# A two-block transformer kernel on one core: the second block's tail as tasks, its first up products by token rows, and several orders rewritten

## The chip, the cores and the metric

The kernel runs on one core of a Trainium2 chip. The core has a matrix engine (TensorE, PE in the profile, with its weight loads as PEld), a vector engine (VectorE, DVE), a scalar engine (ScalarE, ACT), a general one (GpSimd, POOL), and SyncE (SP), which here issues the DMA transfers. Each engine works off its own queue in order, and waits where an operand is not there yet. The metric is the device time of one execution in microseconds (us); the kernel before has a median of 1060.82 us over three runs (1060.1 to 1063.39).

## The reference

One sequence of 256 tokens, 1024 wide, in f32, passes through two blocks. Each block is modulated by vectors that come from a conditioning vector `c`: six vectors of 1024 for each block.

```python
# first block (hybrid_layer)
mod = silu(c) @ ada_w + ada_b
sh1, sc1, gt1, sh2, sc2, gt2 = split(mod, 6)
h = rmsnorm(x, mix_pre_g) * (1 + sc1) + sh1
z, xbc, dt_raw, sc_b, sc_c, sc_h, gates = split(h @ w_in)
y_ssd = ssd_branch(z, xbc, dt_raw, ...) @ w_ssd_out      # chunked scan, chunks of 128 tokens
y_sc = (sc_b * causal_dwconv(sc_c * sc_h, sc_conv_w)) @ w_sc_out
x = x + gt1 * rmsnorm((g_ssd * y_ssd + g_sc * y_sc) @ w_o, mix_post_g)
h = rmsnorm(x, ffn_pre_g) * (1 + sc2) + sh2
u_gate, u_val = split(causal_dwconv(h @ w_up, ffn_conv_w, ffn_conv_b))
x = x + gt2 * rmsnorm((silu(u_gate) * u_val) @ w_down, ffn_post_g)
# second block, "the companion" (hybrid_layer_2)
shift_a, scale_a, gate_a, shift_f, scale_f, gate_f = split(silu(c_2) @ w_ada_2 + b_ada_2, 6)
h = rms_norm(x, attn_norm) * (1 + scale_a) + shift_a
o_a = nsa_mixer(...)       # 8 heads: compressed, selected and windowed keys
o_b = mla_mixer(...)       # 8 heads from low-rank q and kv
x = x + gate_a * ((g_a * o_a + g_b * o_b) @ w_o_2)
h = rms_norm(x, ffn_norm) * (1 + scale_f) + shift_f
val, gt = split(causal_conv3(h @ w_up_2) + b_conv)       # 2 x 2816 channels
x = x + gate_f * ((silu(gt) * val) @ w_down_2)
```

In the kernel the companion's vectors are called sha, sca, ga, shf, scf, gf, in this order.

## The kernel before, in words

**Weights.** All weights are f32 and pass once from DRAM, in halves of 128x1024 values (512 KB), into `raw` buffers (six of them) on SP's queue. ACT rounds each half to the matrix format (`hi`), DVE makes the rest (`lo` = `raw` minus `hi`); five pairs may be held at a time (`HALVES`). Activations exist as such pairs too (`h3h` and `h3l`, `h4h` and `h4l`, `osh` and `osl`, and so on). Each product is then three matrix products: hi by hi, lo by hi, hi by lo. Two forms occur: in the one the weights are stationary and all 256 tokens move, so the result has channels on the partitions; in the other a token tile of 128 is stationary and 512 weight columns move, so the result has tokens on the partitions.

**Order.** A planner in Python (`_Order`, from line 258) writes the program. Pieces of work are generators ("tasks") with a rank (`RANK`); `charge` adds an estimated duration to an engine's clock at each instruction, `pump` (line 323) emits the due task of lowest rank between products, and `force` (line 335) emits the earliest when the products wait. What comes out is a fixed order for each engine. The list `keys` (lines 736 to 769) sets the order of the weight chunks: `SSD_ORDER` for the scan, `ATT` for the attention, and `mix_in` (line 754) puts the chunks of a modulation vector between them, every so many chunks. All compute instructions go through line 408, so the profile shows them by tile names.

**Modulation vectors.** Most vectors need eight halves of their weight matrix, and `ada_mul` (line 966) takes each as one dot product on DVE (the instruction on `raw` and `crow`, shown as CUSTOM_DVE_ANT_0 in the profile and as ISA in the order). Those in `ON_PE`, gt2 and gf, are loaded separately: `adp_load` (line 994) puts eight halves into `big` buffers, `adp_add` (line 1006) sums part of them on DVE, seven of the eight for gf, and `adp_fill` (line 1023) ends the sum with f32 products on TensorE, which also spread it over all partitions.

**Tails.** Behind w_o, w_down and w_o_2 a "tail" scales the result by its gate, adds it to the residual `xr`, takes the norm, turns the tile to channels on partitions, applies scale and shift and makes the next `h` pair. `tail` (line 1495) emits it step by step from hand-written lists (`TAILS`): `mul` and `upd` on DVE, `sqx` on ACT, `nrm`, `diag` (a diagonal matrix `btok` of the norms), `turn` (f32 products of `xr` with `btok`, which scale and transpose in one), `evA` and `evV` (evictions with scale and shift on ACT or DVE), `hi`, `lo`. `out_proj` (line 677) runs the products ahead of it: the last two chunks are held, so that token tile 0 is ready ahead of tile 1.

**The end of the attention.** `mla_task` (line 2207) makes softmax rows `Sm` and `om`; sums go to `oA`, `os_task` (line 2414) splits them into `osh` and `osl`, the operand of w_o_2. Its first two chunks need only the first half of the heads, so their products lie between the last attention pieces. Then come the ga tail, up2 with 22 pairs of channel blocks (`ffn`, line 1671) and dn2.

Of the kernel before, what the change touches and what calls it, by code (L numbers as in the profile page):

```python
# [28 lines left out]
ON_PE = ("gt2", "gf")  # L29


def _plan():
# [70 lines left out]
    for i in range(22):  # L103
        plan.append((("up2", i), 2048, a_pair("w_up_2", 128 * i, 2816 + 128 * i)))
# [102 lines left out]
def _consts():  # L207
# [10 lines left out]
    for dim, s in ((128, ""), (64, "64")):  # L218
# [195 lines left out]
def _body(ctx: ExitStack, tc: tile.TileContext, wst, pf_d, rows_d, cst_d, xT_d, x_d, w2_d, out_d):  # L414
# [86 lines left out]
    st = {"dma": 0, "cast": 0, "half": 0, "ahead": 0}  # L501
# [23 lines left out]
    def cast_next():  # L525
# [30 lines left out]
    def caster():  # L556
        while st["cast"] < 2 * len(keys):
            yield lambda: st["ahead"] < limit[0] and st["cast"] in raws
# [118 lines left out]
    def out_proj(name, nch, x, ready, tail_of, done=lambda c: None):  # L677
# [12 lines left out]
        for c in range(nch - 2):  # L690
            ready(c, 0)
            ready(c, 1)

# [4 lines left out]
            done(c)  # L698
        held = []
        for c in (nch - 2, nch - 1):  # L700
# [3 lines left out]
        for t in range(2):  # L704
            for c in (nch - 2, nch - 1):
                ready(c, t)
            for j in range(2):
                for w, c, hf in held:
# [1771 lines left out]
```

## Time and profile before

| | |
|---|---|
| median of three runs | 1060.82 us (1060.1 to 1063.39) |
| the profiled execution, its own time | 1063.29 us |
| its span, first to last instruction | 1061.5 us |
| mean granted clock of TensorE | 0.988 |
| PE busy | 1027.2 us (97%) |
| PEld busy | 945.2 us (89%) |
| DVE busy | 847.2 us (80%) |
| ACT busy | 625.8 us (59%) |
| POOL busy | 37.1 us (3%) |
| DMA | 234.01 MB, mean 220 GB/s |

The profile is one execution. "Busy" counts the time in which an engine had an instruction in work. Matrix products overlap, so the price of one is read from start to start of a run of them, and not from its duration. The granted clock of a stretch is 1.00 at 2.4 GHz and 0.50 at 1.2 GHz. A row of the list of instructions may join several of one kind (x4), and "[2.79 <-ACT h4h L408]" says that the engine was idle for 2.79 us before it and that ACT's instruction on h4h ended the wait.

### The profile page before, as it was taken

How to read it: one execution, taken by the hardware profiler on the slowest of the kernel's cores; microseconds unless marked ns; L12 is line 12 of the kernel's file. 1: busy time of each engine (PE TensorE's matmuls, PEld its weight loads, DVE VectorE, ACT ScalarE, POOL GpSimd, SP SyncE). 2: the span in 40 equal slices, each digit the busy share in tenths (PEclk: the TensorE clock that was granted, in tenths of full speed). 3: DMA queues.
4: the chain of work that ended last, by engine and by line, in shares of the span. 5: the costliest groups of instructions: out<-in, count | busy, mean ns of one | idle time of the engine just before them, and what ended most of it. 6: DMA issues, size and time to landing. Idle time of an engine off the chain costs nothing.

```text
span 1061.5 us, 18723 instructions
## 1 busy us (share of the span) xinstructions
PE 1027.2 (97%) x7101; PEld 945.2 (89%) x7101; DVE 847.2 (80%) x1557; ACT 625.8 (59%) x1228; POOL 37.1 (3%) x59
## 2 busy tenths in 40 slices
PE   9899999999999999999998989998999789999998
PEld 8889999989999979999987779887998679999986
DVE  5888897978987867989886898997889677877843
ACT  4466577467754456656555467777764346666531
POOL 0000000000000000000000010221100000000000
PEclk8999999999999999999999999998999899999999
DMA  9955496657868947686785688853256716555551
GB/s 354 350 197 182 160 308 230 233 197 267 288 216 275 329 139 235 231 274 203 230 310 186 210 303 292 299 178 131 100 177 232 283 54 206 181 180 183 194 179 40
DMA packets 66186, 234.01 MB, mean 220 GB/s; under 512 B 7568, under 2 KB 8624, under 8 KB 65584
## 3 DMA queue, kind: packets, MB, share of 16 engines
q1 hardware_dynamic: 66096, 232.82, 64.1%
q8 instruction: 55, 0.90, 0.3%
q14 instruction: 35, 0.29, 0.1%
HBM read 230.67 MB, written 2.13 MB: 219 GB/s over the span
## 4 chain that ended last, share of the span: by engine, by line
PE 66%; DVE 6%; ACT 4%; issue 2%; DMA 1%; POOL 0%; SPq 0%; ACTq 0%; DVEq 0%; POOLq 0%
PE ps L408 66%; DVE lo L408 2%; DMA adp<-in_wst_dram 1%; ACT hi L408 1%; ACT S L408 1%; DVE raw L408 1%; DVE S L408 1%; ACT jk L408 0%; DVE jk L408 0%; DVE ropet L408 0%; ACT junk L408 0%; DVE qo L408 0%; DVE Sm L408 0%; POOL ssk L408 0%; DVE tmp L408 0%
## 5 line engine op out<-in xcount | busy, mean ns | idle before, releaser
L408 DVE TENSOR_TENSOR lo<-raw,hi 128x1024 fp32r<-128x1024 f32 (+3 forms) x326 | 387.4, 1195 | 153.0 <-ACT hi L408 150.5
L408 ACT CAST hi<-raw 128x1024 fp32r<-128x1024 f32 (+3 forms) x326 | 331.7, 1030 | 210.2 <-PE ps L408 153.9
L408 PE MATMUL ps<-hh,hi 128*128 128x256 f32 (+1 forms) x520 | 150.4, 291 | 3.1 <-ACT hh L408 3.1
L408 PE MATMUL ps<-hl,hi 128*128 128x256 f32 (+1 forms) x520 | 146.9, 284 | 0.7 <-DVE hl L408 0.2
L408 PE MATMUL ps<-hh,lo 128*128 128x256 f32 (+1 forms) x520 | 146.5, 283 | 0.1
L408 PEld LDWEIGHTS ps<-hh,hi 128*128 128x128 f32 (+1 forms) x520 | 98.6, 190 | 6.6 <-ACT hh L408 5.0
L408 PE MATMUL ps<-h4h,hi 128*128 128x256 f32 x352 | 99.8, 286 | 2.8 <-ACT h4h L408 2.8
L408 PEld LDWEIGHTS ps<-hl,hi 128*128 128x128 f32 (+1 forms) x520 | 98.7, 190 | 3.7 <-DVE hl L408 2.0
L408 PE MATMUL ps<-h4h,lo 128*128 128x256 f32 x352 | 99.6, 286 | 0.0
L408 PEld LDWEIGHTS ps<-hh,lo 128*128 128x128 f32 (+1 forms) x520 | 98.6, 190 | 0.4 <-DVE lo L408 0.3
L408 PE MATMUL ps<-h2h,hi 128*128 128x256 f32 x352 | 98.4, 283 | 0.0
L408 PE MATMUL ps<-h2h,lo 128*128 128x256 f32 x352 | 98.3, 283 | 0.0
L408 PE MATMUL ps<-h2l,hi 128*128 128x256 f32 x352 | 94.7, 283 | 0.0
L408 PE MATMUL ps<-h4l,hi 128*128 128x256 f32 x352 | 94.5, 283 | 0.0
L408 DVE CUSTOM_DVE_ANT_0 raw<-raw,crow 128x1024 f32<-128x1024 f32 x64 | 76.9, 1217 | 0.0
L408 DVE SCALAR_TENSOR_TENSOR fc<-ps,pf,fc 128x254 f32<-128x254 f32 (+1 forms) x176 | 72.3, 473 | 0.0
L408 PEld LDWEIGHTS ps<-h4h,hi 128*128 128x128 f32 x352 | 68.7, 195 | 3.0 <-ACT h4h L408 3.0
L408 PEld LDWEIGHTS ps<-h4h,lo 128*128 128x128 f32 x352 | 68.7, 195 | 0.0
L408 PEld LDWEIGHTS ps<-h2h,hi 128*128 128x128 f32 x352 | 67.6, 192 | 0.8 <-ACT h2h L408 0.8
L408 PEld LDWEIGHTS ps<-h2h,lo 128*128 128x128 f32 x352 | 67.6, 192 | 0.0
L408 PEld LDWEIGHTS ps<-h2l,hi 128*128 128x128 f32 x352 | 65.4, 192 | 0.0
L408 PEld LDWEIGHTS ps<-h4l,hi 128*128 128x128 f32 x352 | 65.4, 192 | 0.0
(393 smaller groups left out, 2330.8 us busy)
## 6 DMA issues: line engine op xcount, KB each, us to landing
raw<-in_wst_dram SPq DMA_DIRECT2D x364, 512.0 KB, 5.0
adp<-in_wst_dram SPq DMA_DIRECT2D x16, 512.0 KB, 7.3
ada0a<-in_wst_dram SPq DMA_DIRECT2D x8, 512.0 KB, 9.0
ada0b<-in_wst_dram SPq DMA_DIRECT2D x8, 512.0 KB, 9.1
E<-scr SPq DMA_DIRECT2D x4, 1024.0 KB, 8.8
raw<-in_wst_dram SPq DMA_DIRECT2D x8, 400.0 KB, 8.9
raw<-in_wst_dram SPq DMA_DIRECT2D x8, 384.0 KB, 8.8
brow<-in_rows_dram SPq DMA_DIRECT2D x4, 512.0 KB, 8.3
```

What stands on the lines that cost most here:

```text
L408: return f(*a, **k)
```

## The change

- gf is no longer in `ON_PE`. Its eight halves go through the weight stream as dot products on DVE, mixed into up2 from chunk 10, and eight small f32 products spread the result (`cst,mod_gf`). The separate loads, seven DVE steps and four wide f32 products of gf go.
- The ga tail is written as tasks (`tail_tasks`). ACT and DVE scale the rows by their norm into `tmp`, and eight plain transposes for each token tile (`cst,tmp`) take the place of the products with `btok`.
- w_o_2 holds all four chunks: token tile 0 runs over all of them, then tile 1. Halves beyond the five pairs go to `big` buffers (`whi`, `wlo`).
- The first four pairs of channel blocks of up2 come as two "windows" of token-row products (weights 512 wide, moving; new layout "up2b"): tile 0 for both windows, then tile 1. Four ACT copies (`ux`) and 16 transposes bring the result to channels on partitions; the rest is as before (`ffn2`).
- The order of the scan's chunks, of some attention chunks, the mixing of sc2, sha, sca, scf and shf, the ranks of many tasks, and a few steps in the lists of gt1 and gt2 are rewritten. shf moves from the attention's start into dn of the first block; scf's eight dot products come in a row.

```diff
-ON_PE = ("gt2", "gf")
+ON_PE = ("gt2",)
...
-    for i in range(22):
+    for p in range(2):
+        cols = np.concatenate([np.arange(256) + o + 256 * p for o in (0, 2816)])
+        for h in range(2):
+            plan.append((("up2b", p, h), 2048, b_list("w_up_2", 4 * h, 4, cols)))
+    for i in range(4, 22):
         plan.append((("up2", i), 2048, a_pair("w_up_2", 128 * i, 2816 + 128 * i)))
...
+SPARED = 3
+RANK_TAIL = (-1.5, -1.2)
...
+            inner = st["hl"] < HALVES
+            if inner:
+                h, l = hlp.tile([128, 1024], F32R, name="hi"), hlp.tile([128, 1024], F32R, name="lo")
+                st["hl"] += 1
+            else:
+                h, l = big("whi", F32R), big("wlo", F32R)
+                O.keep("big", 2)
+            home[i, hf] = inner
...
-    def out_proj(name, nch, x, ready, tail_of, done=lambda c: None):
+    def out_proj(name, nch, x, ready, tail_of, done=lambda c: None, hold=2, spared=None):
...
+        more[0] = spared
         held = []
-        for c in (nch - 2, nch - 1):
+        for c in range(nch - hold, nch):
             def mm(w, hf, c=c):
                 held.append((w, c, hf))
             step((name, c), mm, hold=True)
         for t in range(2):
+            for w, c, hf in held[:-4]:
+                if not hf:
+                    ready(c, t)
+                if not t:
+                    arrive(w, hf)
+                half(t, w, c, hf)
+                if t:
+                    drop(w.i, hf)
+                    if hf:
+                        done(c)
...
-    SSD_ORDER = [(x[:-1], int(x[-1])) for x in "z0 xs1 sc0 sc1 xs2 z1 sc2 sc3 z2 xs3 z3".split()]
+    SSD_ORDER = [(x[:-1], int(x[-1])) for x in "xs1 sc0 xs2 sc1 z0 z1 sc2 sc3 z2 xs3 z3".split()]
...
-    keys += [("up2", i) for i in range(22)] + [("dn2", k) for k in range(11)]
+    keys += [("up2b", p, h) for p in range(2) for h in range(2)] + [("up2", i) for i in range(4, 22)] + [("dn2", k) for k in range(11)]
...
-    mix_in("scf", ("q1", 1), 1)
-    mix_in("shf", ("ns", 0), 2)
+    mix_in("scf", ("q1", 1), 0)
+    mix_in("shf", ("dn", 2), 3)
+    mix_in("gf", ("up2", 10), 3)
...
+    def tail_tasks(gname, post, name, a, sh):
...
+        def tail_task(t, ps):
...
+            r = norm_sum(ss)
+            yield
+            par(lambda: AC.activation(tmp[:, :512], x[:, :512], AF.Identity, scale=r),
+                lambda: VE.tensor_scalar(tmp[:, 512:], x[:, 512:], r, None, op0=OP.mult))
...
+            for f in range(8):
+                transpose(tp[f // 4][:, 128 * (f % 4):128 * (f % 4) + 128], tmp[:, 128 * f:128 * f + 128])
+            yield
...
+            par(lambda: ev(True), lambda: ev(False))
...
+    def windows(names, x, ks, done):
...
+        for t in range(2):
+            O.until(lambda: len(ks) > t and ks[t].done)
+            for n in range(2):
+                ps = bank()
+                for q, (w, hf) in enumerate(held[n]):
+                    arrive(w, hf)
+                    for k in range(2):
...
+                        PE.matmul(ps, xh, w.hi(c, 512), start=kk == 0, stop=False)
+                        PE.matmul(ps, xh, w.lo(c, 512), start=False, stop=False)
+                        x.come(kk, 1, (t,))
+                        PE.matmul(ps, xl, w.hi(c, 512), start=False, stop=kk == 7)
...
+    def ffn2(up, dn, hh, k_hh, w, b_, first_is_gate, tail_of, f):
...
-    h4, k_h4, of = tail("ga", False, "h4", "scf", "shf", "gf")
-    adp("gf", 2)
-    out_proj("wo2", 4, osum, wo2_ready, of)
+    h4, k_h4, of = tail_tasks("ga", False, "h4", "scf", "shf")
+    out_proj("wo2", 4, osum, wo2_ready, of, hold=4, spared=SPARED)
```

Where instructions stand now. First TensorE at the ga tail, from the last w_o_2 products on; before:

```order
L408 MATMUL ps_91<-hi,osl_9205 128x512
L408 MATMUL ps_94<-btok,xr_9131 128x128 x4
L408 MATMUL ps_89<-btok,xr_9131 128x128 x4
L408 MATMUL ps_93<-adp,cb 128x512
L408 MATMUL ps_88<-adp,cb 128x512
L408 MATMUL ps_93<-adp,ones 128x512
L408 MATMUL ps_88<-adp,ones 128x512
L408 MATMUL ps_87<-btok,xr_9133 128x128 x4
L408 MATMUL ps_90<-btok,xr_9133 128x128 x4
L408 MATMUL ps_92<-h4h_9452,hi 128x256
```

After, with buffer numbers (`tmp_9327` is token tile 0's scaled row block; `osh1` and `osl1` are the operands of the last two chunks, here for tile 1; `hi` and `whi` are halves in the five pairs and in `big`):

```order
L408 MATMUL ps6_93<-cst_84,tmp_9327 128x128 x4
L408 MATMUL ps0_87<-cst_84,tmp_9327 128x128 x4
L408 MATMUL ps3_90<-whi_9251,osh1_9144 128x512
L408 MATMUL ps3_90<-wlo_9252,osh1_9144 128x512
L408 MATMUL ps3_90<-whi_9251,osl1_9145 128x512
L408 MATMUL ps3_90<-whi_9277,osh1_9144 128x512
L408 MATMUL ps3_90<-wlo_9278,osh1_9144 128x512
L408 MATMUL ps3_90<-whi_9277,osl1_9145 128x512
L408 MATMUL ps3_90<-whi_9285,osh1_9144 128x512
L408 MATMUL ps3_90<-wlo_9286,osh1_9144 128x512
L408 MATMUL ps3_90<-whi_9285,osl1_9145 128x512
L408 MATMUL ps1_88<-whi_9294,h4h0_9435 128x512
```

The 32 instructions on `btok` and the four on `adp` are gone, tile 0's transposes stand among tile 1's products with nine products behind them, and the first product of `h4h` moves 512 weight columns.

Second, DVE at the end of the attention, from the last-but-one `om`; before:

```order
L408 TENSOR_SCALAR Sm<-Sm,sumsm 128x256
L408 SCALAR_TENSOR_TENSOR om<-sgate,ps_88 128x512
L408 SCALAR_TENSOR_TENSOR adp<-adp,cact 128x1024
L408 TENSOR_SCALAR Sm<-Sm,sumsm 128x256
L408 TENSOR_TENSOR oA_7521<-oA_7521,om 128x4x128
L408 COPY Sm<-ps_94 128x256
L408 SCALAR_TENSOR_TENSOR adp<-adp,cact 128x1024
L408 TENSOR_TENSOR osl_9205<-oA_7521,osh_9204 128x4x128
L408 SCALAR_TENSOR_TENSOR om<-sgate,ps_89 128x512
```

After:

```order
L408 SCALAR_TENSOR_TENSOR om<-sgate,ps_93 128x512
L408 TENSOR_SCALAR Sm<-Sm,sumsm 128x256
L408 TENSOR_TENSOR oA_7521<-oA_7521,om 128x4x128
L408 COPY Sm<-ps_87 128x256
L408 TENSOR_TENSOR wlo<-raw,whi 128x1024
L408 TENSOR_TENSOR osl_9145<-oA_7521,osh_9144 128x4x128
L408 SCALAR_TENSOR_TENSOR om<-sgate,ps_88 128x512
L408 SCALAR_TENSOR_TENSOR oA_7521<-sgate,ps_91 128x2x128
L408 TENSOR_TENSOR oA_7521<-oA_7521,om 128x4x128
L408 TENSOR_TENSOR wlo<-raw,whi 128x1024
L408 TENSOR_TENSOR osl_9145<-oA_7521,osh_9144 128x4x128
L408 TENSOR_TENSOR wlo<-raw,whi 128x1024 x4
```

The `adp` steps between `om` and `Sm` are gone; casts of held weights (`wlo`) stand there instead, behind the last `Sm`.

Third, DVE behind the gt2 tail, at the start of the attention (`h3l` ends the tail, `kc` are keys to be compressed); before:

```order
L408 TENSOR_TENSOR h3l_6431<-tmp,h3h_6430 128x4x128
L408 TENSOR_TENSOR lo<-raw,hi 128x1024
L408 ISA raw,mod_shf<-raw,crow 128x1024
L408 ISA mod_shf 128x1
L408 ISA raw,mod_shf<-raw,crow 128x1024
L408 ISA mod_shf 128x1
L408 TENSOR_TENSOR lo<-raw,hi 128x1024
L408 TENSOR_TENSOR kc_6555<-ps_89,rot 128x256
```

After:

```order
L408 TENSOR_TENSOR h3l_6457<-tmp,h3h_6456 128x4x128
L408 TENSOR_TENSOR lo<-raw,hi 128x1024 x4
L408 TENSOR_TENSOR kc_6580<-ps_88,rot 128x256
L408 TENSOR_TENSOR ropet<-ps_88,rot 128x2x64 x2
L408 TENSOR_TENSOR kc_6580<-kc_6580,ropet 128x256
L408 TENSOR_TENSOR lo<-raw,hi 128x1024
```

The dot products of shf are gone from this place; the casts of the weights stand alone.

## Rows read from the trace of the kernel before

**Rows 1.** PE's list of instructions: start, duration, instruction, idle before and its releaser.
```profile
229.10 0.39 PE L408 MATMUL ps<-yscl,hi 128*128 128x256 f32 x1 [1.65 <-DVE yscl L408]
...
327.65 0.39 PE L408 MATMUL ps<-yTl,hi 128*128 128x256 f32 x1 [1.00 <-DVE yTl L408]
...
583.70 0.50 PE L408 MATMUL ps<-hi,h3h 128*128 128x512 f32 x1 [2.85 <-ACT h3h L408]
...
592.76 0.50 PE L408 MATMUL ps<-hi,h3h 128*128 128x512 f32 x1 [1.27 <-ACT h3h L408]
...
624.15 0.44 PE L408 MATMUL ps<-cst,ko 128*128 128x128 f32 x2 [2.54 <-DVE ko L408]
...
729.69 0.69 PE L408 MATMUL ps<-cst,S 128*128 128x128 f32 x2 [1.79 <-ACT kxn L408]
...
843.00 0.69 PE L408 MATMUL ps<-cst,Sm 128*128 128x128 f32 x2 [4.83 <-DVE Sm L408]
...
868.69 0.48 PE L408 MATMUL ps<-h4h,hi 128*128 128x256 f32 x1 [2.79 <-ACT h4h L408]
```

**Rows 2.** Stages: span, busy PE PEld DVE ACT POOL, granted clock, DMA share, GB/s.
```profile
520.00:580.00 60.00, 60.00 (x270) 49.61 (x269) 44.02 (x71) 28.62 (x45) 1.08 (x2) 1.00 0.73 246
...
728.90:735.70 6.80, 5.35 (x20) 4.49 (x21) 4.01 (x16) 5.88 (x23) 1.27 (x2) 0.50 0.24 86
...
841.50:848.40 6.90, 5.39 (x22) 5.11 (x23) 5.61 (x8) 0.62 (x1) 0.00 (x0) 0.51 1.02 414
...
868.80:872.20 3.40, 3.40 (x17) 3.40 (x18) 2.07 (x2) 3.19 (x4) 0.00 (x0) 0.50 0.11 39
872.20:1000.00 127.80, 127.80 (x1055) 127.27 (x1055) 101.44 (x174) 81.42 (x131) 0.00 (x0) 1.00 0.56 188
```

**Rows 3.** PE's list, the w_o_2 products and the ga tail.
```profile
848.95 0.40 PE L408 MATMUL ps<-hi,osh 128*128 128x512 f32 x1
...
858.50 1.95 PE L408 MATMUL ps<-btok,xr 128*128 128x128 f32 x16
860.28 1.88 PE L408 MATMUL ps<-adp,cb 128*128 128x512 f32 x4
862.00 1.88 PE L408 MATMUL ps<-adp,ones 128*128 128x512 f32 x4
863.85 2.05 PE L408 MATMUL ps<-btok,xr 128*128 128x128 f32 x16
```

**Rows 4.** PE's list: four transposes, and 32 products of 256 columns.
```profile
824.75 0.60 PE L408 MATMUL ps<-cst,S 128*128 128x128 f32 x4
825.11 0.70 PE L408 MATMUL ps<-hi,osh 128*128 128x512 f32 x2
...
877.95 4.00 PE L408 MATMUL ps<-h4l,hi 128*128 128x256 f32 x32
881.79 0.28 PE L408 MATMUL ps<-h4h,hi 128*128 128x256 f32 x1
```

**Rows 5.** ACT's list at the ga tail.
```profile
860.48 1.50 ACT L408 ACTIVATE tmp<-ps,mod_shf,mod_scf 128x128 f32<-128x128 f32 x4
...
862.47 0.62 ACT L408 CAST h4h<-tmp 128x512 fp32r<-128x512 f32 x1
...
864.03 1.04 ACT L408 CAST hi<-raw 128x1024 fp32r<-128x1024 f32 x1
```

**Rows 6.** DVE's list at the attention's end.
```profile
837.99 0.69 DVE L408 SCALAR_TENSOR_TENSOR om<-sgate,ps 128x512 f32<-128x512 f32 x1 [0.32 <-PE ps L408]
841.40 1.28 DVE L408 SCALAR_TENSOR_TENSOR adp<-adp,cact 128x1024 f32<-128x1024 f32 x1 [2.72 <-DMA adp<-in_wst_dram]
842.60 0.35 DVE L408 TENSOR_SCALAR Sm<-Sm,sumsm 128x256 f32<-128x256 f32 x1
```

**Rows 7.** The page's costliest groups: casts to lo, and dot products.
```profile
L408 DVE TENSOR_TENSOR lo<-raw,hi 128x1024 fp32r<-128x1024 f32 (+3 forms) x326 | 387.4, 1195 | 153.0 <-ACT hi L408 150.5
...
L408 DVE CUSTOM_DVE_ANT_0 raw<-raw,crow 128x1024 f32<-128x1024 f32 x64 | 76.9, 1217 | 0.0
```

More of the change, by code (lines that the diff above doesn't have):

```diff
@@ L500, in _body @@
     raws, parts, landed, cast_at = {}, {}, {}, {}
-    st = {"dma": 0, "cast": 0, "half": 0, "ahead": 0}
+    st = {"dma": 0, "cast": 0, "half": 0, "ahead": 0, "hl": 0}
+    home, more, limit = {}, [None], [HALVES]
     units = []
@@ L557, in caster @@
         while st["cast"] < 2 * len(keys):
-            yield lambda: st["ahead"] < limit[0] and st["cast"] in raws
+            yield lambda: st["cast"] in raws and (st["hl"] < limit[0] or more[0] is not None and O.used["big"] + 2 + more[0] <= CAP["big"])
             O.cur.now = max(landed[st["cast"]], free_at[0] if st["ahead"] == HALVES - 1 else 0.0)
@@ L707, in out_proj @@
             for j in range(2):
-                for w, c, hf in held:
+                for w, c, hf in held[-4:]:
                     if not t and not j:
@@ new lines, in windows @@
+    def windows(names, x, ks, done):
+        held = [[], []]
+        for n, nm in enumerate(names):
+            for ch in range(2):
+                step((*nm, ch), lambda w, hf: held[n].append((w, hf)), hold=True)
+        for t in range(2):
[5 more added lines that the diff above has]
+                    for k in range(2):
+                        kk = 2 * q + k
+                        O.pump()
+                        x.come(kk, 0, (t,))
+                        xh, xl = x.hi(kk, 128 * t, 128), x.lo(kk, 128 * t, 128)
+                        c = hf * 1024 + k * 512
+                        PE.matmul(ps, xh, w.hi(c, 512), start=kk == 0, stop=False)
+                        PE.matmul(ps, xh, w.lo(c, 512), start=False, stop=False)
+                        x.come(kk, 1, (t,))
+                        PE.matmul(ps, xl, w.hi(c, 512), start=False, stop=kk == 7)
+                    if t:
+                        drop(w.i, hf)
+                    elif n and q == 3:
+                        more[0] = None
+                done(n, t, ps)
@@ L1669, in up_task, with copy_task, turn_task, done @@
         yield from f.split(i, 1, g)
+    def ffn2(up, dn, hh, k_hh, w, b_, first_is_gate, tail_of, f):
+        ks, ux, k_tr = {}, {}, []
+        def copy_task(n, t, ps):
+            yield from room(a2=1)
+            ux[n, t] = a2("ux")
+            O.keep("a2")
+            AC.copy(ux[n, t], ps)
+            free(ps)
+            yield
+        def turn_task(n, k):
+            yield k
+            O.adopt("a2", 2)
+            pss = []
+            for i in range(2):
+                b = yield from tbank()
+                pss.append(b)
+            for i in range(2):
+                for j in range(2):
+                    for t in range(2):
+                        transpose(ab(pss[i], j)[:, 128 * t:128 * t + 128], ux[n, t][:, 256 * j + 128 * i:256 * j + 128 * i + 128])
+            O.rel("a2", 2)
+            yield
+            for i in range(2):
+                ks[2 * n + i] = O.spawn(up_task(2 * n + i, pss[i], w, b_, first_is_gate, f))
+        def done(n, t, ps):
+            k = O.spawn(copy_task(n, t, ps), -0.7)
+            if t:
+                k_tr.append(O.spawn(turn_task(n, k), -0.6))
+        windows([(up + "b", p) for p in range(2)], hh, k_hh, done)
+        O.rel("big")
+        for i in range(4, 22):
+            ks[i] = O.spawn(up_task(i, chunk_a((up, i), hh), w, b_, first_is_gate, f))
+        hh.drop()
+        O.drain(*k_tr)
+        out_proj(dn, 11, f, lambda c, t: O.drain(ks[2 * c], ks[2 * c + 1]), tail_of, lambda c: c % 2 and f.drop_part(c // 2))
+        f.drop()
     def ffn(up, dn, hh, k_hh, w, b, first_is_gate, tail_of):
         f = HL("f")
+        if up == "up2":
+            return ffn2(up, dn, hh, k_hh, w, b, first_is_gate, tail_of, f)
         ks, held = [], [[], []]
```

114 lines of the change are left out of this document (96 added, 18 removed), and 3 rows, old and new, of the table TAILS.

## The prediction

> **What bounds the kernel now.** The table by engine comes first: TensorE is busy for 1027.2 of a span of 1061.5 us, DVE for 847.2. So TensorE's own work is the bound nearly everywhere, and a change can gain in three ways only: less work on TensorE, fewer stalls of it, less time at its lower clock. The second view is the list of TensorE's instructions with the idle time ahead of each. Its stalls sum to some 29 us, and eight of them [rows 1] hold 18.7 us: two in the scan (1.65 and 1.00, both for a low half that DVE makes), two behind the gt2 tail (2.85 and 1.27, for h3h from ACT), one of 2.54 for `ko`, one of 1.79 in the attention's front, 4.83 at the attention's end for `Sm`, 2.79 behind the ga tail for h4h. The third view is the table by stage with the granted clock [rows 2]: 1.00 nearly throughout, but 0.50 or 0.51, the level of 1.2 GHz, in three short stretches from 728.9, 841.5 and 868.8 us. Each lies behind one of those stalls; but after the 2.85 at 583.70 and the 2.54 at 624.15 no such stretch follows, so a stall of that size alone does not bring it. Work at half the clock takes twice as long: half the busy time of such a stretch is lost. 2.7 of the 5.39 us from 841.5, 1.7 of the 3.40 from 868.8, and 2.7 of the 5.35 from 728.9.
>
> All sums below go against the profiled execution: 1063.29 us, which is its span of 1061.5 and 1.8 around it. The median of the runs shown, 1060.82, lies 2.5 below it, so I take the same difference off the median.
>
> **a. TensorE's own work.** Gone are the four f32 products of 128x512 that made gf: from 860.28 to 863.85 us, 3.57 us [rows 3]. Gone are the 16 diagonal products of the ga tail (two of the listed instructions each): 858.50 to 860.28 is 1.78 us for the first token tile's eight, 0.22 each, so 3.56. New are eight f32 products that spread the finished gf over the partitions; at that 0.22 they cost 1.8. New are 32 transposes, 16 of the tail and 16 of the `ux` tiles; four took 0.36 us from 824.75 to 825.11 [rows 4], so 0.09 each and 2.9 in all. The first four channel blocks of up2 change from 192 products that move 256 columns to 96 that move 512: 32 of the one kind take 3.84 us (877.95 to 881.79 [rows 4]), 0.12 each; 42 of the other take 9.55 us (848.95 to 858.50 [rows 3]), 0.227 each. That is 23.0 against 21.8, so −1.2. Sum: −3.57 −3.56 +1.8 +2.9 −1.2 = **−3.6**.
>
> The Trainium skill ("TensorE: Matmul & The Clock Gate", Back-to-back issue gap) states for one isolated product the columns at 2.4 GHz plus about 2.5 ns. That would be 109 ns and 216 ns, and the new widths would save 0.2 us instead of 1.2. The rows are 11 ns above it at both widths, so the fixed part is larger here and the wider form gains more; by the page the forecast would be 1.0 us higher, which changes no chance.
>
> **b. The ga tail.** Before, DVE and ACT have nothing but the second tile's diagonal products to hide the first tile's tail, and TensorE stalls 2.79 us for h4h at 868.69 [rows 1], then runs 3.40 us at half clock [rows 2]. After, all four chunks of w_o_2 are held, and each token tile is finished for all of them in turn. Behind tile 0 stand 39 products ahead of its transposes, 39 × 0.227 = 8.9 us, against some 3.5 us of tail (two multiplies and adds, a square, a scaling), so the transposes wait for nothing, even with the three weight casts that stand between (3.6 [rows 7]). Behind the transposes only 9 products are left, 2.0 us, ahead of the first h4h product. On ACT stand there four 128x128 evictions, 1.50, one weight cast, 1.04, and the h4h cast, 0.62 [rows 5]: 3.2 us. So a wait of 1.2 for h4h, and some 0.4 for the low half that follows it: +1.6. Ends: 0 if the cast slips ahead, 4 if DVE's weight cast before h4l is late as well. The second tile's tail lies beside the windows' first-tile products, 48 × 0.227 = 10.9 us, and costs nothing; without that cover it would be the same 3 us. I drop the half clock (1.7), since 1.6 us is below stalls here that brought none. Sum: −2.79 −1.7 +1.6 = **−2.9**.
>
> **c. The attention's end.** TensorE waits 4.83 us for `Sm` [rows 1]. On DVE the scaling of Sm at 842.60 stands behind an `adp` instruction that waits 2.72 us for its DMA and takes 1.28 [rows 6]; `om` before it was done by 838.7. With adp("gf") gone, Sm can follow at 838.7: −3.9, and without that stall no half clock follows: −2.7. What is late next: before, the 48 products of the first two chunks for both tiles lay between the attention's last pieces. After, only 24 do (5.4 us); the other 24, of tile 1, come after. So up to 5.4 us of waits that were filled may open. I take half, +2.7, because the last pieces before did have 4.8 us open in spite of all 48. And tile 0's products of the last two chunks now need low halves (`wlo`) whose casts stand on DVE among the last pieces: from the last attention product on, DVE has `om`, two sums into `oA` (one of them half as wide), a `wlo`, `osl` and the last `wlo`. With om's 0.69 [rows 6] for each of the four, less 0.3, and 1.195 for each cast [rows 7] that is 4.9 us; TensorE has 11 products, 2.5, to fill it. The rest is a new wait, +2.5, ends 0 (the casts slip ahead) and 5 (nothing fills). Sum: −3.9 −2.7 +2.7 +2.5 = **−1.4**.
>
> **d. The scan.** The new chunk order (xs1 and xs2 ahead of sc0 and sc1, z0 and z1 later) and the ranks move DVE's work. Counted over the order, with each instruction at its duration of before, DVE has 13.6 us less ahead of the last `yscl` at the same work of TensorE, and 7.5 us less ahead of the last `yTl`. Stalls of 1.65 and 1.00 [rows 1] are smaller than that: **−2.65**.
>
> **e. The wait for ko.** Before, DVE makes four dot products of shf between the gt2 tail and `ko`, 4 × 1.217 = 4.9 us [rows 7]. They now lie in the dn products, where DVE is busy 44.0 of 60 us [rows 2], so it has the room. From the tail's h3l to ko DVE then has 20.2 us of work instead of 25.5 and TensorE 2.2 us more: 2.54 goes, **−2.5**.
>
> **f. Kept, or at nothing.** The gt2 tail's two stalls (4.1) stay: its steps hardly move. The attention's front from 700 to 736 keeps its stalls (1.79 and some 2 us of smaller ones) and its half clock, 6.5 in all: q00 comes later and the ranks of nearly all its tasks change, so this may go to 0 or double; I take 0 as the change, ends −6.5 and +6.5. The eight scf dots now stand in a row, 8 × 1.217 [rows 7], 9.7 us, while the four halves of the last q chunk, 12 products of 512 columns each, cover 10.9 us of TensorE: nothing, or up to 2 us where fewer halves are ready. The eight gf dots lie in up2, where DVE is busy 101.4 of 127.8 us [rows 2], and so do the four copies on ACT (81.4): 9.7 us more fit. SP issues eight `raw` loads there in the place of eight `adp` loads: the same bytes, out of the stretch of 841 us where the DMA share is 1.02, into one at 0.56 [rows 2].
>
> **The sum.** −3.6 −2.9 −1.4 −2.65 −2.5 = −13.05: 1050.2 for the profiled execution, **1048** for the median.
>
> **Rivals.**
> 1. *The gain is spent at the attention's end* (same or a little faster). The filler is lost whole (+2.7 more), the late low halves cost 5 instead of 2.5 (+2.5), and both half clocks come back (+2.7, +1.7), since a stall only moves. Then −13.05 + 9.6 = −3.5, 1057. For it: TensorE and DVE both run near 80% there, and the stall at 843 was reached with 48 products of fill. Against it: DVE loses six adp steps there, 7.7 us.
> 2. *The attention starves* (slower). With half the filler and with q00 later, TensorE waits for each of the last softmax pieces: +5.4 for the fill, 5 for the low halves, 6.5 for the front doubled, and two half-clock stretches like that of 841.5 at 2.7. With what c counts already taken off, 2.7 + 2.5 + 6.5 + 5.4 = 17.1 on the forecast's −13.05, so +4: 1065. It decides once these waits sum to some 16 us more than I counted, 13.05 and the 3.2 that can be measured. For it: the attention is where TensorE has nothing else to do, and the old stalls cluster there. Against it: in the front the weights' products still alternate with it.
> 3. *The front comes free too* (more gain). The later q00 leaves DVE and ACT free for the compressed keys, and the 6.5 us from 700 to 736 go: −19.55, 1041.3.
> 4. *The order does nothing in d and e*: the waits are for something else in the chain, and 5.2 stays: 1053. This is within the range of the forecast.
>
> **How the numbers follow.** The forecast with rival 4 has 0.64, from 1043 to 1055 by the bounds of b and c. Rival 3 has 0.09, rival 1 has 0.16, rival 2 has 0.11. The range of 8 in 10 reaches from a little under rival 3's time, 1040, up to 1062, between rivals 1 and 2. A measurement of this kernel tells about 0.3%, 3.2 us: 1057.6 and 1064.0 are the marks. Faster: 0.64 + 0.09 + a little under a third of rival 1 (0.04) = 0.77. Same: the rest of rival 1 and a little of rival 2, 0.13. Slower: 0.10.
>
> **What would show it.** In the profile after: no stall over 1 us ahead of yscl, yTl or ko; no adp between om and Sm on DVE, and ahead of Sm on TensorE under 1.5 us; products of `wlo` with waits of 2 to 3 us in all; h4h products of tile 0 with 1 to 2 us of wait, those of tile 1 with none; the granted clock at 1.00 from 860 on; 96 products of `h4h` at 0.227. It would be wrong if TensorE's busy time fell by less than 3 us at the full clock, if the stretch from the first q products to the end of w_o_2 grew by more than 5 us, or if a row of scf dots left TensorE without halves.

## The result and the profile after

The changed kernel takes 1050.19 us, the median of four runs (1048.98 to 1051.54), against 1062.11 for the kernel before beside it (1060.1 to 1063.67): ratio 0.988, 95% interval 0.9862 to 0.9898. Run again in a later group it took 1051.37, ratio 0.9881 (0.9859 to 0.9902). The forecast was 1048 in a range of 1040 to 1062, so time and direction came out as said. What was inside the sum did not, and that the total fits is in part luck: the parts that I had credited with most of the gain bring the smaller share when they are made alone, and two stretches that I had put at nothing moved by several us, in opposite directions.

The page of the profile after, its head and the busy time of the engines:

```profile
span 1049.0 us, 18536 instructions
PE 1020.2 (97%) x7013; PEld 937.4 (89%) x7013; DVE 849.6 (81%) x1566; ACT 626.4 (60%) x1233; POOL 40.6 (4%) x59
```

To see where 12.5 us of span went, lay the two lists of TensorE's instructions side by side and read where the products of each kind start. The work between two such marks is the same in both but for what the change removes or adds there.

| from the first product of ... to the first of ... | before | after | difference | forecast |
|---|---|---|---|---|
| span's start to the end of the last hh product (projections, scan) | 309.98 | 308.71 | −1.27 | −1.65 |
| from there to mixh (scan's end) | 50.21 | 48.11 | −2.10 | −1.00 |
| mixh to h2h (gt1 tail) | 31.82 | 34.41 | +2.59 | 0 |
| h2h to h3h (first FFN, gt2 tail) | 191.69 | 191.69 | 0.0 | 0 |
| h3h to h4h (attention, ga tail) | 284.99 | 270.45 | −14.54 | −11.9 |
| h4h to TensorE's end (second FFN) | 188.33 | 191.12 | +2.79 | +1.5 |
| to the span's end | 4.50 | 4.49 | 0.0 | 0 |

The forecast column is the prediction's terms put where they act: 8 of the 32 transposes and 1.2 of the 1.6 us wait fall ahead of the first h4h product, the rest behind it.

TensorE's stalls after, the ones that answer to [rows 1]: in the gt1 tail, at the gt2 tail, at `ko`, through the attention, and at the ga tail (start, duration, instruction, idle before it and who ended it).

```profile
379.63 2.05 PE L408 MATMUL ps<-btok,xr 128*128 128x128 f32 x16 [0.86 <-DVE btok L408]
386.55 2.05 PE L408 MATMUL ps<-btok,xr 128*128 128x128 f32 x16 [1.43 <-DVE btok L408]
391.23 0.38 PE L408 MATMUL ps<-h2h,hi 128*128 128x256 f32 x1 [0.91 <-ACT h2h L408]
...
582.92 0.50 PE L408 MATMUL ps<-hi,h3h 128*128 128x512 f32 x1 [2.85 <-ACT h3h L408]
...
593.61 0.50 PE L408 MATMUL ps<-hi,h3h 128*128 128x512 f32 x1 [1.27 <-ACT h3h L408]
...
624.39 0.38 PE L408 MATMUL ps<-cst,ko 128*128 128x128 f32 x2
...
649.50 0.38 PE L408 MATMUL ps<-lo,h3h 128*128 128x256 f32 x1 [0.68 <-DVE lo L408]
...
687.28 0.30 PE L408 MATMUL ps<-lo,blkv 128*30 128x256 f32 x1 [0.93 <-DVE lo L408]
...
690.95 0.50 PE L408 MATMUL ps<-lo,cqTh 128*128 128x512 f32 x1 [0.75 <-DVE lo L408]
...
812.41 0.73 PE L408 MATMUL ps<-hi,osl 128*128 128x512 f32 x2 [1.68 <-DVE osl L408]
...
826.88 0.41 PE L408 MATMUL ps<-cst,Sm 128*128 128x128 f32 x2 [0.81 <-DVE Sm L408]
...
835.78 0.50 PE L408 MATMUL ps<-wlo,osh 128*128 128x512 f32 x1 [1.35 <-DVE wlo L408]
837.51 0.50 PE L408 MATMUL ps<-wlo,osh 128*128 128x512 f32 x1 [0.78 <-DVE wlo L408]
...
853.37 0.50 PE L408 MATMUL ps<-whi,h4h 128*128 128x512 f32 x1 [0.59 <-ACT h4h L408]
853.71 0.40 PE L408 MATMUL ps<-wlo,h4h 128*128 128x512 f32 x1
854.71 0.50 PE L408 MATMUL ps<-whi,h4l 128*128 128x512 f32 x1 [0.61 <-DVE h4l L408]
```

The waits ahead of yscl and yTl are gone, `ko` no longer waits, and the 4.83 us for `Sm` are 0.81 at most. In their place are a few waits for low halves, `lo` in the front and `wlo` at the end, all under 1.4 us, and three in the gt1 tail where the kernel before has one of 0.56. The wait of 1.68 for `osl` is hardly new: the kernel before waits 0.90 and 0.61 for it.

The attention's middle is told by the table by stage: span, then busy PE, PEld, DVE, ACT, POOL, then the granted clock. First the kernel before:

```profile
700.00:740.00 40.00, 35.87 (x219) 30.27 (x219) 30.33 (x124) 30.68 (x122) 6.62 (x14) 0.91 0.35 119
740.00:770.00 30.00, 29.87 (x213) 26.87 (x212) 24.82 (x104) 22.30 (x93) 2.81 (x5) 1.00 0.26 90
```

and the changed kernel:

```profile
700.00:740.00 40.00, 39.21 (x262) 34.20 (x261) 35.29 (x139) 34.23 (x147) 6.33 (x12) 1.00 0.41 131
740.00:770.00 30.00, 30.00 (x223) 27.99 (x221) 23.79 (x95) 21.80 (x85) 2.65 (x4) 1.00 0.32 104
```

From 700 to 740 us TensorE is busy 3.3 us longer in the same 40, at the full clock: this is the front that I had left as it was.

### The profile page after: what moved, and what is told of

The parts are those of the page before. It is cut to its first block, busy times and chain, and to the rows that moved or that the text cites. A ratio compares the mean times of both kernels' runs of the same rounds, so it can differ in the third digit from the quotient of the medians.

```text
span 1049.0 us, 18536 instructions
## 1 busy us (share of the span) xinstructions
PE 1020.2 (97%) x7013; PEld 937.4 (89%) x7013; DVE 849.6 (81%) x1566; ACT 626.4 (60%) x1233; POOL 40.6 (4%) x59
## 4 chain that ended last, share of the span: by engine, by line
PE 55%; ACT 4%; DVE 3%; issue 1%; DMA 1%; POOL 0%; DVEq 0%; ACTq 0%
PE ps L408 55%; DVE lo L408 1%; ACT hi L408 1%; ACT S L408 1%; ACT jk L408 1%; DMA raw<-in_wst_dram 1%; ACT Sm L408 0%; DVE raw L408 0%; DVE tmp L408 0%; ACT Sc L408 0%; DVE Sm L408 0%; ACT junk L408 0%; DVE wlo L408 0%; DVE S L408 0%; DVE osl L408 0%
## 5 line engine op out<-in xcount | busy, mean ns | idle before, releaser
L408 DVE TENSOR_TENSOR lo<-raw,hi 128x1024 fp32r<-128x1024 f32 (+2 forms) x319 | 379.3, 1195 | 138.0 <-ACT hi L408 135.6
L408 ACT CAST hi<-raw 128x1024 fp32r<-128x1024 f32 (+2 forms) x319 | 324.2, 1030 | 190.9 <-PE ps L408 120.8
L408 DVE CUSTOM_DVE_ANT_0 raw<-raw,crow 128x1024 f32<-128x1024 f32 x72 | 86.0, 1218 | 0.0
L408 PE MATMUL ps<-h4h,hi 128*128 128x256 f32 x280 | 79.4, 284 | 0.0
L408 PE MATMUL ps<-h4l,hi 128*128 128x256 f32 x280 | 79.2, 283 | 0.0
L408 PE MATMUL ps<-h4h,lo 128*128 128x256 f32 x280 | 79.2, 283 | 0.0
L408 ACT ACTIVATE fc<-ps,pf 128x256 f32<-128x256 f32 x88 | 45.5, 561 | 37.5 <-PE ps L408 20.4
L408 PE MATMUL ps<-hi,fh 128*128 128x512 f32 x176 | 56.8, 389 | 0.0
L408 PE MATMUL ps<-lo,fh 128*128 128x512 f32 x176 | 56.8, 389 | 0.0
```

The lines of the kernel that those rows point to most:

```text
L408: return f(*a, **k)
```

## The experiments

Eleven edited kernels ran in three groups, and the changed kernel once more in the last of them. A ratio is to the kernel before in the same group; where two kernels of different groups are compared, the difference is taken from their ratios. For the attention, the next table splits the stretch from the first h3h to the first h4h product: its length, TensorE's idle time in it, what the half clock took (half of the busy time in stretches at 1.2 GHz, an estimate that the last section checks), and the rest, which is work. It has the kernels whose gain or loss lies mainly there.

| kernel | median us | ratio (95%) | h3h to h4h | idle | half clock | rest |
|---|---|---|---|---|---|---|
| before | 1062.1 | 1 | 285.0 | 18.5 | 5.4 | 261.1 |
| changed | 1050.19 | 0.9880 (0.9862 to 0.9898) | 270.5 | 11.9 | 3.4 | 255.2 |
| e_struct | 1060.31 | 0.9974 (0.9960 to 0.9989) | 280.8 | 16.9 | 8.5 | 255.4 |
| e_orders | 1054.76 | 0.9917 (0.9890 to 0.9943) | 277.7 | 13.4 | 3.4 | 260.8 |
| e_gf | 1059.64 | 0.9973 (0.9954 to 0.9992) | 278.9 | 17.8 | 3.1 | 258.0 |
| e_shf | 1065.08 | 1.0020 (1.0002 to 1.0039) | 281.6 | 19.1 | 7.4 | 255.2 |
| e_att | 1057.79 | 0.9955 (0.9941 to 0.9968) | 276.9 | 14.6 | 6.0 | 256.3 |
| e_rank | 1075.47 | 1.0116 (1.0082 to 1.0149) | 297.4 | 25.7 | 13.8 | 257.9 |
| e_scf | 1051.69 | 0.9884 (0.9858 to 0.9910) | 271.0 | 10.7 | 6.3 | 254.0 |

**The structure alone.**

```diff
 # the changed kernel, with ATT, RANK, SSD_ORDER, the lists of gt1 and gt2,
 # and mix_in of sc2, sha, sca, scf and shf as before
```

> The changed kernel with all orders set back: scan chunks, attention chunks, ranks, the mixing of sc2, sha, sca, scf and shf, and the step lists of gt1 and gt2 are those of before; gf in the stream, the ga tail as tasks and the windows stay. Theory (the structure brings what TensorE's own work, the ga tail and the end of the attention are worth, the orders the rest): -3.6 -2.9 -1.4 and no more, so about 8 us under the kernel before, ratio 0.9925, and the stalls ahead of yscl, yTl and ko are back at 1.6, 1.0 and 2.5 us, with the gt1 tail again at one stall of 0.6. Rival (the structure brings all, the orders move stalls from place to place): 12 us under before, ratio 0.988.

Measured: ratio 0.9974, a gain of 2.7 us where my theory had 8 and the rival 12. The old stalls are back as said (yscl 1.65, yTl 1.00, ko 2.53, gt1 0.57). The work that the structure takes from the attention and its tail is all there, 261.1 to 255.4. But idle time and half clock in the stretch are not less, 23.9 before and 25.4 here, so it is only 4.2 us shorter, and the second FFN is 3.1 longer. In this run the same stall as before at the gt2 tail (2.85 us at 583.61) was followed by a stretch at the lower clock, which it was not in the kernel before:

```profile
585.10:588.50 3.40, 3.40 (x9) 2.67 (x8) 2.78 (x4) 2.26 (x5) 0.80 (x2) 0.50 0.55 178
```

And at the attention's end `Sm` still waits. The adp instruction is gone, but two casts of held w_o_2 halves now stand on DVE in its place, ahead of `om` and `Sm`; behind the wait the clock is 0.50 for 3.4 us from 841.1. DVE's rows, then TensorE's:

```profile
836.77 2.35 DVE L410 TENSOR_TENSOR wlo<-raw,whi 128x1024 fp32r<-128x1024 f32 x2
839.04 0.68 DVE L410 SCALAR_TENSOR_TENSOR om<-sgate,ps 128x512 f32<-128x512 f32 x1
839.64 0.35 DVE L410 TENSOR_SCALAR Sm<-Sm,sumsm 128x256 f32<-128x256 f32 x1
```

```profile
840.04 0.44 PE L410 MATMUL ps<-cst,Sm 128*128 128x128 f32 x2 [2.76 <-DVE Sm L410]
```

**The orders alone.**

```diff
 # the kernel before, with the new ATT, RANK, SSD_ORDER, lists of gt1 and gt2,
 # and mix_in of sc2, sha, sca, scf and shf; gf and the ga tail as before
```

> The kernel before with the new orders alone (scan chunks, attention chunks, ranks, mixing of the vectors, step lists of gt1 and gt2); gf by separate loads and the old ga tail stay. Theory: the scan gains 2 us, the gt1 tail loses 2.6, the attention's front gains some 3 to 6 (its half-clock stretch goes), the stall of 4.8 us for Sm stays; in all 4 us under before, ratio 0.996. Rival (the orders bring nothing by themselves): 0 to 1 us, ratio 0.999 to 1.000.

Measured: ratio 0.9917, 8.8 us: twice what I expected, and three times the structure's gain. One reason is that the stall of 4.8 us for `Sm`, which I had let stay, is not there. The adp instructions still stand on DVE, but in the new order the only one ahead of `osl` that waits for its DMA waits 0.47 us (835.05), and TensorE's largest waits at the attention's end are these two:

```profile
833.04 0.49 PE L400 MATMUL ps<-Sm,vb 128*128 128x128 f32 x2 [1.36 <-DVE Sm L400]
...
837.64 0.80 PE L400 MATMUL ps<-hi,osh 128*128 128x512 f32 x1 [2.12 <-ACT osh L400]
```

The two ratios multiplied give 0.989 against 0.988 for the whole, so within their intervals the shares add up: about a quarter is structure, three quarters are orders. Each on top of the other, by the ratios, the structure is worth 3.9 us and the orders 10.

**gf alone through the weight stream.**

```diff
-ON_PE = ("gt2", "gf")
+ON_PE = ("gt2",)
     mix_in("shf", ("ns", 0), 2)
+    mix_in("gf", ("up2", 10), 3)
...
-    h4, k_h4, of = tail("ga", False, "h4", "scf", "shf", "gf")
-    adp("gf", 2)
+    h4, k_h4, of = tail("ga", False, "h4", "scf", "shf", None)
```

> The kernel before with gf alone moved to the weight stream: no separate loads, eight dot products on DVE in up2, eight small products; tail steps, windows and orders as before. Theory (the adp transfer on DVE's queue made the 4.83 us wait for Sm): TensorE -3.57 +1.8, the wait for Sm falls under 1.5 us (-3.9), its half clock goes (-2.7): 8 us under before, ratio 0.992. Rival (Sm waits for the softmax chain anyway, the adp step only stood in the gap): -1.8 alone, ratio 0.998.

Measured: ratio 0.9973, 2.9 us, nearer the rival's size, though the theory's mechanism holds. DVE's list first, then TensorE's:

```profile
838.39 0.69 DVE L408 SCALAR_TENSOR_TENSOR om<-sgate,ps 128x512 f32<-128x512 f32 x1 [0.32 <-PE ps L408]
838.99 0.35 DVE L408 TENSOR_SCALAR Sm<-Sm,sumsm 128x256 f32<-128x256 f32 x1
```

```profile
839.40 0.44 PE L408 MATMUL ps<-cst,Sm 128*128 128x128 f32 x2 [0.83 <-DVE Sm L408]
...
852.38 1.95 PE L408 MATMUL ps<-btok,xr 128*128 128x128 f32 x16
857.73 2.05 PE L408 MATMUL ps<-btok,xr 128*128 128x128 f32 x16 [3.41 <-DVE btok L408]
862.57 0.39 PE L408 MATMUL ps<-h4h,hi 128*128 128x256 f32 x1 [2.79 <-ACT h4h L408]
```

Sm follows om at once and the wait falls from 4.83 [rows 1] to 0.83, the 3.9 us of my term, and no half-clock stretch follows it. But the 3.57 us of gf products [rows 3] had stood between the two tiles' diagonal products, while DVE and ACT made the second norm. Without them TensorE waits 3.41 us for that norm. Work taken out of the middle of a dependent tail turned into a stall of nearly its own length.

**No windows in up2.**

```diff
         if up == "up2":
-            return ffn2(up, dn, hh, k_hh, w, b, first_is_gate, tail_of, f)
+            more[0] = None
+            O.until(lambda: len(k_hh) > 1 and k_hh[0].done and k_hh[1].done)
```

> The changed kernel without the two windows of up2: all 22 pairs of channel blocks have both token tiles moving, and wait until both tail tasks are done. Theory (the windows cost TensorE about 1 us of work and buy the cover of the second tile's tail): the second tail stands open, a stall of 5 to 7 us ahead of the first h4h product, so 4 to 6 us slower than the changed kernel, 1055. Rival (the cover is worth nothing since the tail could hide behind w_o_2): same as the changed kernel within 1 us.

The plan and the keys have all 22 pairs in the old form again. Measured: 1060.48, ratio 0.9965 (0.9949 to 0.998), some 9 us slower than the changed kernel; the stall is longer than I had put it, since the second tail starts only behind the last w_o_2 product, and the clock is 0.50 for 10.2 us from 857.2, in the stall and behind it:

```profile
861.05 1.97 PE L404 MATMUL ps<-cst,tmp 128*128 128x128 f32 x8 [7.67 <-ACT tmp L404]
```

The work from the first h4h product to the first of dn2, less idle time and half clock, is 128.4 us here and 130.5 in the changed kernel, 2.1 more, with 24 transposes in it. Eight of these are the second tile's tail, and here they stand ahead of the first h4h product, where this kernel has 1.3 us more work. So the windows themselves cost TensorE about 1 us, as the theory had it, and buy the cover of this stall.

**Single orders set back in the changed kernel.** The list of the gt1 tail:

```diff
-... next: sq:1,0 mul:1,0 diag:0 turn:0 fill:4 sq:1,1 nrm:1,0 mul:1,1 evA:0,0,0,1,2,3 ...
+... next: sq:1,0 diag:0 sq:1,1 turn:0 mul:1,0 fill:4 nrm:1,0 mul:1,1 evA:0,0,0,1,2,3 ...
```

> The changed kernel with the step list of the gt1 tail as before. Theory (the reordered list opens the three stalls of 0.86, 1.43 and 0.91 us between 378 and 391 us, where before there was one of 0.57): the list set back takes them away, 2.6 us under the changed kernel, about 1047.5, ratio 0.986 to the kernel before. Rival (the stalls come from the ranks and from the denser mixing of sha, not from the list): they stay, 1050, ratio 0.988.

Measured: 1046.89, ratio 0.9854 (0.9827 to 0.988): the theory's side, and faster than both kernels. The stall is one again:

```profile
379.62 2.05 PE L406 MATMUL ps<-btok,xr 128*128 128x128 f32 x16 [0.57 <-DVE btok L406]
```

The changed kernel's list of DVE shows how the first of the three opens: `mul:1,0` for tile 1 stands ahead of `btok` for tile 0, for which TensorE waits. The other two follow on the second tile's side, whose steps are reordered too.

```profile
378.69 0.69 DVE L408 TENSOR_TENSOR tmp<-ps,brow 128x512 f32<-128x512 f32 x1 [0.16 <-ACT jk L408]
379.30 0.28 DVE L408 TENSOR_SCALAR btok<-cst,r 128x128 f32<-128x128 f32 x1
```

The place of shf:

```diff
-    mix_in("shf", ("dn", 2), 3)
+    mix_in("shf", ("ns", 0), 2)
```

> The changed kernel with shf mixed in at the attention's start again, every second chunk behind the first ns chunk. Theory (DVE's dot products there make the wait for ko and keep DVE behind through the front): the stall of 2.5 us ahead of ko is back, the lo waits of 0.6 to 0.9 us between 648 and 691 us stay or grow, 2.5 to 5 us slower than the changed kernel, ratio 0.990 to 0.993. Rival (the wait only moved from ko to the lo casts behind it): within 1 us of the changed kernel, since the 2.9 us of lo waits go as the 2.5 us come back.

Measured: 1065.08, ratio 1.002, some 15 us slower than the changed kernel, three times what my theory had. The wait for ko is back, but most of the loss comes over 100 us later. TensorE's list at ko, and the stages behind:

```profile
623.57 0.69 PE L408 MATMUL ps<-cst,ko 128*128 128x128 f32 x2 [2.55 <-DVE ko L408]
```

```profile
700.00:740.00 40.00, 38.14 (x254) 33.66 (x253) 31.47 (x118) 33.58 (x143) 7.34 (x16) 1.00 0.39 130
740.00:770.00 30.00, 25.80 (x160) 22.78 (x159) 22.11 (x79) 15.46 (x48) 3.57 (x5) 0.83 0.31 106
```

From 740 to 770 us it does 160 listed instructions where the changed kernel does 223. A granted clock of 0.83 there is 10.2 us at 0.50, from 745.9 on, and ahead of it TensorE waits 1.91 us at 744.69. Another 3.0 us are lost in the second FFN (194.1 us against 191.1), where a stretch at 0.50 follows the ga tail.

The attention's chunk order, and the ranks:

```diff
-ATT = "w1k0 w1k1 cm0 bg0 cm1 w1k2 w1k3 w1v0 ckv0 q00 w1v1 ..."
+ATT = "w1k0 w1k1 cm0 bg0 cm1 w1k2 q00 w1k3 w1v0 ckv0 w1v1 ..."
```

> The changed kernel with the attention's chunk order of before (q00 ahead of w1k3 and w1v0). Theory (the later q00 is what frees the attention's front and takes its stalls and half clock away): the stalls ahead of S and kcT from 700 to 736 us are back at 3 us and more, 4 us slower than the changed kernel, ratio 0.992. Rival (the ranks do it, the place of q00 is worth nothing): within 1 us of it, ratio 0.988.

```diff
-RANK = {'row_task': -0.5, 'ada_task': 0.5, ..., 'nsa_task': 1.0, 'mla_task': -0.5}
+RANK = {"row_task": -0.5, "ada_task": 0, ..., "nsa_task": 1.5, "mla_task": -0.5}
```

> The changed kernel with the table of task ranks of before, all else as changed. Theory (the place of q00 does it, the ranks only shift small stalls): within 1.5 us of the changed kernel, ratio 0.987 to 0.989. Rival (the ranks of the attention's tasks bring the gain of about 8 us that the orders alone gave there): 6 to 8 us slower than the changed kernel, ratio 0.994 to 0.996.

Measured: 1057.79 for the old place of q00, some 8 us slower than the changed kernel, and 1075.47 for the old ranks, 25 us slower and slower than the kernel before. Both theories that gave the gain to one of the two fall: each is needed. With the old q00 the stalls don't come back where I said, at 700 to 736 us, but at the end, 2.61 ahead of osl at 820 and 1.85 and 1.47 ahead of Sm, with 6.8 us at 0.50 from 818.7 on. With the old ranks TensorE has 13.8 us more idle time and 10.4 more of half clock in the attention (the table above). The stretch that collapses first is the one that shf also spoils, again with 10.2 us at 0.50:

```profile
700.00:740.00 40.00, 37.46 (x243) 32.13 (x242) 29.68 (x119) 32.10 (x138) 7.04 (x12) 1.00 0.34 114
740.00:770.00 30.00, 25.04 (x151) 21.39 (x150) 18.41 (x65) 15.04 (x54) 3.23 (x3) 0.83 0.21 70
```

The scan's order, and the row of scf dots:

```diff
-    SSD_ORDER = ... "xs1 sc0 xs2 sc1 z0 z1 sc2 sc3 z2 xs3 z3"
+    SSD_ORDER = ... "z0 xs1 sc0 sc1 xs2 z1 sc2 sc3 z2 xs3 z3"
```

> The changed kernel with the scan's chunk order of before. Theory (the chunk order takes the two scan stalls away): the stalls of 1.65 us ahead of yscl and 1.00 ahead of yTl are back and the new one of 0.65 at 137 us goes; 2.1 us slower than the changed kernel, ratio 0.990. Rival (the ranks of the scan's tasks did it): they stay away, ratio 0.988.

```diff
-    mix_in("scf", ("q1", 1), 0)
+    mix_in("scf", ("q1", 1), 1)
```

> The changed kernel with the four scf chunks one apart again behind the second q1 chunk, as before. Theory (eight dot products in a row or spread cost the same, since held halves cover them): within 1 us of the changed kernel, ratio 0.987 to 0.989. Rival (spread out, they stand on DVE between the attention's front pieces and hold them up, as the earlier q00 did): 4 to 8 us slower, ratio 0.992 to 0.996.

Measured: the scan's old order gives 1056.22, ratio 0.9929 (0.99 to 0.9957), 5 us slower than the changed kernel run beside it. Neither theory holds: the stall ahead of yscl does not return, that ahead of yTl is 0.30, and a new one stands between, for the scaled `xs`, with a half-clock stretch behind it, so that the stretch from the last hh product to mixh is 7.2 us longer (55.3 against 48.1) and the attention 2.4 shorter:

```profile
326.56 2.15 PE L408 MATMUL ps<-cst,xs 128*128 128x128 f32 x8 [2.83 <-DVE xs L408]
```

The run with the old ranks, e_rank, tells the other half: with the new chunk order it has neither of the two stalls, and 48.1 us for the same stretch. So the chunk order takes them away whichever the ranks, and the ranks alone, without it, bring another.

The scf dots spread out give 1051.69 against 1051.37: the same, as the theory said. The two halves of the attention differ by more than that, but it cancels.

**The changed kernel again.**

> The changed kernel once more, unaltered, on the chip and in the rounds of the others: about 1050, ratio 0.988. Both theories of the half-clock stretches speak here: if they hang on chance, those between 580 and 660 us differ from the first profile though the stalls are the same; if they hang on the stalls, they come at the same places (583.7 and 652.0).

Measured: 1051.37. The stalls over 1 us are the same, and so are the half-clock stretches at 583.8 and 652.0. But a third one stands at 826, where the first profile had the full clock in the same 3.3 us. First the repeat, then the first profile:

```profile
826.20:829.50 3.30, 3.30 (x17) 3.30 (x16) 1.91 (x5) 0.80 (x2) 0.00 (x0) 0.50 0.00 0
```

```profile
826.20:829.50 3.30, 2.62 (x22) 2.52 (x23) 2.70 (x8) 1.24 (x3) 0.00 (x0) 1.00 0.00 0
```

So neither theory alone: some places draw the lower clock in both executions, at others it comes in one and not in the next. What this third one cost can be read: the attention from its first to its last S product takes 1.5 us longer in the repeat (104.5 against 103.0 from start to start).

**Another gt2 list on top of the gt1 list.**

```diff
-... upd:1,1 cast: done:1,0 evA:0,1,0,1,2 done:0,0 hi:0,0 hi:0,1 lo:0,0 upd:1,0 fill:6 lo:0,1 cast: ...
+... upd:1,1 done:1,0 evA:0,1,0,1,2 done:0,0 hi:0,0 hi:0,1 lo:0,0 upd:1,0 fill:6 lo:0,1 cast: cast: ...
```

> The changed kernel with the gt1 list of before (which gave 1046.9) and, in the gt2 list, one weight cast moved from among the first tile's evictions to behind both low halves. Theory (the cast of 1.05 us on ACT and its 1.2 us on DVE stand ahead of h3h and h3l and are a third of the 2.85 us stall): the stall falls to 1.8 us, 1 us less, 1045.9, ratio 0.9845. Rival (the moved half is then late for the h3h products, or ACT waits for its evictions anyway): the stall stays or comes back behind the first products, 1047, ratio 0.9855.

Measured: 1048.54, ratio 0.9855 (0.9829 to 0.9881). The rival is right: ACT now waits for DVE in the place of the cast. ACT's row, then TensorE's:

```profile
579.33 1.16 ACT L406 ACTIVATE tmp<-ps,mod_sha,mod_sca 128x128 f32<-128x128 f32 x3 [0.80 <-DVE tmp L406]
```

```profile
581.05 0.50 PE L406 MATMUL ps<-hi,h3h 128*128 128x512 f32 x1 [2.82 <-ACT h3h L406]
```

The version that beats both kernels is therefore e_gt1: 0.9854 against 0.988. It was not timed in one group with the changed kernel, and their intervals overlap, but the 2.6 us are read in the trace at the place of the edit (31.83 us from mixh to h2h, and 34.41 in the changed kernel). And e_gt12, which has the same gt1 list, did run beside the changed kernel: 1047.77 to 1049.89 against 1050.23 to 1053.09, so all its runs are faster.

## Why the prediction was right, and where it was not

**a. TensorE's work** was mis-sized: −3.6 was forecast for the two stretches in which the change acts, −2.0 came. From h3h to h4h the rest column falls by 5.9 us, where −3.57 −3.56 and eight transposes make −6.4. From h4h to TensorE's end the work, less idle time and half clock, grows by 3.9 (186.6 to 190.5), where +1.8, 24 transposes and −1.2 for the wider products make +2.8. gf's small products cost 1.8 in up2 as said: from the first h4h product to the first of dn2, e_gf has 128.35 us of work against 126.6 before. The rest is the windows with their transposes: 2.1 us more work against e_nowin, where I had +1.0. Eight `ux` transposes take 0.89 us from start to start, and not 0.72:

```profile
872.32 1.14 PE L408 MATMUL ps<-cst,ux 128*128 128x128 f32 x8
873.21 0.47 PE L408 MATMUL ps<-hi,h4h 128*128 128x512 f32 x1
```

The 512-wide products keep to 0.227, but each restart behind a stall or a transpose takes some 0.1 us more (0.32 from 850.45 to 850.77, where one takes 0.23).

**b. The ga tail** was right in the changed kernel: 0.59 and 0.61 us of wait for h4h and h4l, 1.2 where I had 1.6, none for tile 1, and the clock stays at 1.00 there. That the removal of gf's products needs this cover was not in the prediction; e_gf shows it. Nor was it said that the cover needs the orders: in e_struct the two waits are 1.55 and 0.87.

**c. The attention's end** was right term by term in the changed kernel, where it can be read, and wrong on whose gain it is. Sm's wait behind the adp transfer goes (e_gf), the late `wlo` cost 1.35 + 0.78 = 2.1 where I had 2.5, and the thinner filler shows as waits for Sm of 0.57, 0.62 and 0.81, 2.0 where I had 2.7. But the −3.9 and −2.7 do not come with the structure: e_struct has 2.76 of wait for `Sm` behind the `wlo` casts and a half-clock stretch behind that, while e_orders has no such wait with adp in place.

**d. The scan** was right in direction and a little too small: −3.4 came for −2.65. Idle time is 2.0 of it: the stalls of 1.65 and 1.00 are gone, and one of 0.65 opens at 137 us. The other 1.4 us the trace shows as busy time, and only part of them is traced: around the stall for yTl two products start 1.38 us apart, of which 1.00 counts as idle, while the next ones follow each other every 0.12. All kernels here with the new ranks or the new chunk order have the last hh product 0.9 to 2.0 us earlier, and those with neither do not. Of the two causes that I named, the chunk order is enough for these two stalls (e_rank); without it, the new ranks keep them nearly away and open another (e_ssd).

**e. The wait for ko** went, but the step "2.54 goes" failed as a gain in its place: from h3h to the first S product the stretch grew, 143.8 to 144.6 us. Waits for `lo` of 0.6 to 0.9 between 649 and 691 took 2.9 us, and two half-clock stretches, which the kernel before does not have there, some 3. What the move of shf is worth comes later, as e_shf shows: without it the stretch from 740 to 770 collapses.

**f. "I take 0 as the change"** for the attention's front is the step that failed most. From its first to its last S product the attention is 4.6 us shorter, 107.9 to 103.3, and the front's half clock is gone; rival 3 had this at 6.5. The prediction split the gain into some 8 us of structure and 5 of orders. The runs give 2.7 and 8.8, or 3.9 and 10 each on top of the other. The gt1 tail, +2.6, had no term at all: the prediction does not speak of its list. Attention and scan gained 2.6 and 0.7 us more than forecast, the gt1 tail and up2 lost 2.6 and 1.3 more, and so the total came out within 0.6 us of the forecast change. That these errors cancel is luck.

The prediction's reading of the clock leaves out a fourth stretch: 0.50 for 6.8 us from 8.7 us on, at the program's start. Every kernel here has as much half clock in its first 40 us, so no sum changes by it.

What stays open is why the old ranks cost 25 us together with the rest of the change: single ranks were not tried. Nor were the mixing of sc2, sha and sca, the gt2 list, or the held w_o_2 chunks without the new tail set back alone.

## What to carry to other kernels

Ask of work that you take off the bound engine what waits behind it: in the middle of a dependent chain it may be the cover of the next wait, and its time comes back as idle time unless other work takes its place. An order of tasks that are planned together is one quantity: shf's place, q00's place and the ranks cost some 15, 8 and 25 us when each is set back alone, and all orders set back together cost 10 (e_struct), so such terms can't be added up from single edits. Where a hand-written list of steps changes, check for each step which engine is waited for: a few steps of the next tile moved ahead of it cost 2.6 us here.

## What was not expected of the hardware

The lower clock is not set by the stall alone. Behind the same 2.85 us stall at the gt2 tail, and in the same products, it came in the changed kernel, in its repeat and in e_struct, and not in the kernel before, in e_gt1 or in e_shf; and the repeat had one 3.4 us stretch more, at 826 us, than the first profile of the same kernel. The price can be read between the two h3h waits: 9.06 us from start to start before (583.70 to 592.76 [rows 1]), 10.69 in the changed kernel (582.92 to 593.61), so 1.6 us for a stretch of 3.4, a little under the half of it that the prediction took. Differences of that size between the lengths of two profiles say nothing about a change by themselves: of the 3.6 us by which e_gt1's profile is shorter than the changed kernel's, 1.6 are this stretch.
